# Stage borders of a two-block network: where the second feed-forward tile is converted, and what stands behind the norms

## The chip, the core and the metric

The kernel runs on one core of one Trainium2 chip. The metric is the device time of one execution in microseconds (us), the median of three runs. The engines of a core run beside each other, each works through its own instructions in a fixed order, and they wait for each other by semaphores: TensorE (PE, with its weight load PEld), VectorE (DVE), ScalarE (ACT), GpSimd (POOL), and SyncE (SP), which here issues the weight DMAs.

## The reference

256 tokens of width 1024 go through two transformers of two layers each, in fp32. Each layer is a chain of sub-blocks, and each sub-block begins with an RMS norm and a shift and scale that come from a condition vector. What bears on the change:

```python
mod = (cond @ mod_w[l] + mod_b[l]).reshape(B, 9, D)
h = modulate(rmsnorm(x, norm_g[l, 0]), mod[:, 0], mod[:, 1])
x = x + 0.5 * mod[:, 2][:, None, :] * swiglu(h, ffn_w1[l, 0], ffn_w2[l, 0])
...                       # a mixer (LRU and attention, or NSA), then a second feed-forward
return rmsnorm(x, final_norm_g)          # ends the first transformer

def swiglu(h, w1, w2):
    a, b = jnp.split(h @ w1, 2, axis=-1)
    return (jax.nn.silu(a) * b) @ w2
```

The second transformer has a mixer of four parts, one dense feed-forward and one mixture of eight experts (top 2, width 3584). The change doesn't touch the experts.

## The kernel before

**fp32 as three products.** A matmul in fp32 is made of three: each operand is split into a rounded part and a rest. For weights, `chunk()` (L273 to L303) does it: SP loads 1 MB into a `w` tile (three buffers in turn), ACT writes the rounded part `h` (L301), DVE the rest `lo` (L302), each in two halves of 128x1024. For activations, `split()` (L318 to L320) writes `hhi` on ACT and `hlo` on DVE.

**Order.** The code is traced with a scheduler that chooses each engine's order. Two means bind it: `high_priority()`, and `keep_in_program_order(i)`, which puts instruction i behind the one of the same engine that was traced before it.

**Norm.** `token(t)` (L394 to L399) takes one half of the tokens (128): ACT squares the two halves of X (L341), DVE and POOL make `rstd` (L343, and a power at L344), DVE scales and shifts (`sp<-X,rstd,gate` L383, `sp<-sp,gate` L384), PE transposes (L553) and `split` writes hhi and hlo. In the first mixer of the second transformer, `rstd2` (L350 to L370) joins the final norm of the first transformer with this norm; the normalized X itself is written by ACT (L368) and POOL (L369).

**Feed-forward.** `ffn()` (L471 to L535) runs five times; the traces name them by their places: ffn00, ffn01 (from 346 us), ffn10, ffn11 and ffnb. The width of 2816 is cut into 11 groups of 256 (`j`). Group 0 goes token half by token half as the norms end: `m_tile` with w1 and w3, then `silu` on ACT (L498) and a product `sa` on DVE (L499), whose transposes (`finish`) wait until group 1 has begun. Groups 1 to 10 use `s_form` (L455), weights stationary, 24 matmuls of 256 columns for each 128 columns of weights. After group j comes the down projection of group j-1 with w2, whose tiles come from the pool `own`.

**Modulation steps.** `step()` advances a generator (L189 to L221) that works out later shifts, scales and gates: each step issues two 512 KB loads (`mw`) on SP and two DVE instructions `macc` (L212), 128x1024 each, which are kept in program order. Steps stand between the pieces of the feed-forward groups, and in the two mixers of the first transformer behind each token half of the first projection.

Of the kernel before, what the change touches and what calls it, by code (L numbers as in the profile page):

```python
# [8 lines left out]
FT = mybir.dt.float32  # L9
FR = mybir.dt.float32r  # L10
BF = mybir.dt.bfloat16
I32 = mybir.dt.int32
AF = mybir.ActivationFunctionType
OP = mybir.AluOpType
# [57 lines left out]
class Kernel:  # L72
# [197 lines left out]
        return self.res[key]  # L270


    def chunk(self, src, k, n, own=None, perm=False):  # L273
        nc = self.nc
        raw = self.turn_of(self.raw)
        if isinstance(raw, tuple):

            rr = [r[:, :k * n // 2] for r in raw]
        else:
            rr = [raw.tile([128, 2048], FT, name="w")[:, :k * n]]  # L280
        kk = k // len(rr)
        for i, r in enumerate(rr):
            nc.sync.dma_start(r.rearrange("p (k n) -> p k n", k=kk), src[:, i * kk:i * kk + kk])
        hv, lv = [(own or self.turn_of(pools)).tile([128, 2048], FR, name=name)[:, :k * n]
                  for pools, name in ((self.hip, "h"), (self.lop, "lo"))]
        if perm:

            cut = lambda z, e: z.rearrange("p (k " + e + " v) -> p a k x v", k=k, x=2, a=2)
            for a in range(2):
                o = [cut(z, "a x")[:, a] for z in (hv, lv)]  # L290
                i = cut(rr[0], "x a")[:, a]
                nc.scalar.activation(o[0], i, AF.Copy)
                nc.vector.tensor_sub(o[1], i, o[0].bitcast(FT))
        parts = 0 if perm else max(self.parts, len(rr))
        for x in range(parts):
            d = k * n // parts
            xs = slice(x * d, x * d + d)
            i = x * len(rr) // parts
            at = x * d - i * kk * n
            r = rr[i][:, at:at + d]  # L300
            nc.scalar.activation(hv[:, xs], r, AF.Copy)  # L301
            nc.vector.tensor_sub(lv[:, xs], r, hv[:, xs].bitcast(FT))  # L302
        return (hv.rearrange("p (k n) -> p k n", k=k), lv.rearrange("p (k n) -> p k n", k=k))  # L303

    @staticmethod
# [44 lines left out]
    def rstd2(self, xg, t):  # L350


        nc = self.nc
        ss = self.small.tile([128, 4], FT, name="ss2")
        rr = self.small.tile([128, 2], FT, name="rstd2")
        for h in range(2):
            hs = slice(h * 512, h * 512 + 512)
            nc.vector.tensor_mul(xg[:, hs], self.X[t][h], self.before[:, hs])
            for i, x in enumerate((self.X[t][h], xg[:, hs])):
                scr = self.ps.tile([128, 512], FT, name="p")  # L360
                nc.scalar.activation(scr, x, AF.Square, scale=1.0 / 32.0, accum_out=ss[:, 2 * i + h:2 * i + h + 1])
        nc.vector.tensor_scalar(rr[:, 0:1], ss[:, 0:1], ss[:, 1:2], EPS, op0=OP.add, op1=OP.add)
        nc.vector.tensor_add(ss[:, 2:3], ss[:, 2:3], ss[:, 3:4])
        nc.vector.scalar_tensor_tensor(rr[:, 1:2], rr[:, 0:1], EPS, ss[:, 2:3], op0=OP.mult, op1=OP.add)
        nc.gpsimd.tensor_tensor(rr, rr, self.mhalf.to_broadcast([128, 2]), OP.pow)
        for h in range(2):
            x = self.X[t][h]
            nc.scalar.activation(x, x, AF.Copy, scale=rr[:, 0:1])  # L368
            nc.gpsimd.tensor_tensor(x, x, self.before[:, h * 512:h * 512 + 512], OP.mult)  # L369
        return rr[:, 1:2]  # L370

    def norm_rows(self, g, sh, t):

# [97 lines left out]
    def ffn(self, name, w1, w3, w2, nkey, gkey, ahead):  # L471
        nc = self.nc
        w1, w3, w2 = self.wview(w1), self.wview(w3), self.wview(w2)
        NG = F // 256
        self.ahead(*ahead)
        sh, g = self.mod(*nkey), self.mod(*nkey[:2], nkey[2] + 1)
        self.ctx_first.close()
        with ExitStack() as ctx:
            wk = self.pool(name, 1, ctx)
            own = self.pool(name + "w", 2, ctx)  # L480
            self.n2 = 9
            c = [self.chunk(w[:, :, 0:256], 8, 256) for w in (w1, w3)]
            h, token = self.norm(g, sh)
            A = self.accs()
            todo, G, late = [], {}, []
            for j in range(NG):
                gh = self.t2(wk, [128, 2, 256], "gh", FR)
                gl = self.t2(wk, [128, 2, 256], "gl", FR)
                if j == 0:

                    for t in range(2):
                        with self.tc.high_priority():
                            token(t)
                        p = self.ps.tile([128, 512], FT, name="p")
                        for i in range(2):
                            self.m_tile(p[:, i * 256:i * 256 + 256], h, c[i], 0, 8, 0, 256, t, True, True)
                        sa = self.t2(wk, [128, 256], "sa")
                        nc.scalar.activation(sa, p[:, :256], AF.Silu)  # L498
                        nc.vector.tensor_mul(sa, sa, p[:, 256:])  # L499

                        def finish(t=t, sa=sa, gh=gh, gl=gl):
                            p = self.transpose4(sa, 2)
                            ts = slice(t * 128, t * 128 + 128)
                            self.split(gh[:, :, ts], gl[:, :, ts], p[:, :256].rearrange("p (k n) -> p k n", k=2))
                        late.append(finish)
                else:
                    c = [self.chunk(w[:, :, j * 256:j * 256 + 256], 8, 256) for w in (w1, w3)]
                    pp = []
                    for i in range(2):
                        p = self.ps.tile([128, 512], FT, name="p")  # L510
                        for t in range(2):
                            self.s_form(p[:, t * 256:t * 256 + 256], h, c[i], t * 128)
                        pp.append(p)
                        for finish in late:
                            finish()
                        late = []
                        if j < NG - 1:
                            self.step()
                    sa = self.t2(wk, [128, 512], "sa")
                    nc.scalar.activation(sa, pp[0], AF.Silu)  # L520
                    nc.vector.tensor_mul(sa, sa, pp[1])
                    self.split(gh, gl, sa.rearrange("p (k n) -> p k n", k=2))
                G[j] = (gh, gl)
                if j == 1:
                    self.late_setup()
                for i in ([j - 1] if j < NG - 1 else [j - 1, j]):
                    if i < 0:
                        continue
                    c = self.chunk(w2[:, 2 * i:2 * i + 2, :], 2, 1024, own)
                    todo += [(G[i], k, c, k) for k in range(2)]  # L530
                if todo:
                    self.down(wk, A, todo, j == 1, j == NG - 1, self.mod(*gkey) if j == NG - 1 else None)
                    todo = []
                if j < NG - 2:
                    self.step()  # L535
# [30 lines left out]
    def mixer0(self):  # L566
        nc = self.nc
        W = self.wview(self.i_mix0_in_w[0])
        with ExitStack() as ctx:
# [49 lines left out]
            def tokens(c0):  # L619
                A = self.accs(2)  # L620
                if not R:
                    c = [weights(c0, kh) for kh in range(2)]
                    for t in range(2):
                        with self.tc.high_priority():
                            token(t)
                        for kh in range(2):
                            self.m_tile(A[t], h, c[kh], 4 * kh, 4, 0, 512, t, kh == 0, kh == 1)
                        self.step()
                        yield
                    return A  # L630
                for kh in range(2):
                    c = weights(c0, kh)
                    self.m_form(A, h, c, 4 * kh, 4, 0, 512, kh == 0, kh == 1)
                    self.step()
                    yield
                return A
# [155 lines left out]
    def mixer1(self):  # L792
# [3 lines left out]
        with ExitStack() as ctx:  # L796
# [7 lines left out]
            for t in range(2):  # L804
                with self.tc.high_priority():
                    token(t)
                for kh in range(2):
                    self.m_tile(A[t], h, c[kh], 4 * kh, 4, 0, 512, t, kh == 0, kh == 1)
                self.step()


            V = [wk.tile([128, 2, 9, 64], FR, name=n) for n in ("vhi", "vlo")]
# [266 lines left out]
    def mixer2(self, l):  # L1079
# [3 lines left out]
        with ExitStack() as ctx:  # L1083
# [31 lines left out]
            def m_proj(c0, name):  # L1115
# [4 lines left out]
                for t in range(2):  # L1120
# [3 lines left out]
                    self.m_tile(A[t], h, c, 0, 8, 0, 256, t, True, True)  # L1124
                    if t == 0:
                        yield
                self.step()
                if name is None:
                    return A
# [575 lines left out]
```

## Time and profile before

| | |
|---|---|
| median of three runs | 2661.75 us (2661.14 to 2663.9) |
| the profiled execution | 2663.27 us, of which the span from first to last instruction is 2661.4 us |
| PE busy | 2555.5 us (96%), 14939 matmuls |
| DVE, ACT, POOL busy | 2170.3 us (82%), 1537.0 us (58%), 207.8 us (8%) |
| mean granted TensorE clock | 0.978 of full speed |
| DMA | 727.33 MB, mean 273 GB/s |

How to read it: PE is busy nearly all of the time, so the kernel's length is the matmuls' time, plus the gaps in PE, plus what a lower clock adds. A gap shows in the timeline as idle time in brackets, with the instruction that ended it. An engine with idle time costs nothing by that alone; what counts is whether PE waits for it at that moment. A stretch's granted clock stands in the table by windows (1.00 is 2.4 GHz, 0.50 is 1.2 GHz).

### The profile page before, as it was taken

The numbers are of one execution on the slowest core, as the hardware profiler recorded it, in microseconds if no ns is written. First come the engines' busy times: TensorE is split into PE (matmuls) and PEld (weight loads), VectorE is DVE, ScalarE is ACT, GpSimd is POOL, SyncE is SP. The second block draws the span as 40 slices with busy tenths as digits, with TensorE's granted clock in tenths as the row PEclk, the third lists the DMA queues.
The fourth block names the chain that finished last, engine by engine and source line by source line (L and its number), as shares of the span: only waits on it lengthen the run. The fifth ranks groups of instructions, "written<-read, shape, count | busy, mean of one in ns | idle before, by whom it ended". The sixth has DMA issues, their size and how long they took to land. (4 is left out here: it accounts for less than half of the span.)

```text
span 2661.4 us, 38016 instructions
## 1 busy us (share of the span) xinstructions
PE 2555.5 (96%) x14939; PEld 2207.7 (83%) x14939; DVE 2170.3 (82%) x2446; ACT 1537.0 (58%) x2026; POOL 207.8 (8%) x236
## 2 busy tenths in 40 slices
PE   8999999999998999899999898999999999999997
PEld 5998789989977899887998776888888887888775
DVE  6877888587478787687886976999999898988887
ACT  3454644444446545455444545777777777777775
POOL 2001200000003100231000221000000000000000
PEclk9999999999999999989999988999999999999999
DMA  9986469769553399454895746999999999999993
GB/s 341 335 310 198 174 228 332 259 216 328 179 199 112 111 320 311 157 184 143 298 323 194 239 156 224 381 347 364 347 375 342 348 350 342 348 351 349 351 343 122
DMA packets 366633, 727.33 MB, mean 273 GB/s; under 512 B 16350, under 2 KB 165072, under 8 KB 366448
## 3 DMA queue, kind: packets, MB, share of 16 engines
q1 hardware_dynamic: 362704, 717.20, 77.0%
q0 software_dynamic: 3712, 7.63, 0.9%
q8 instruction: 119, 1.95, 0.3%
q14 instruction: 66, 0.54, 0.1%
q10 hardware_dynamic: 32, 0.01, 0.0%
HBM read 723.73 MB, written 1.05 MB: 272 GB/s over the span
## 5 line engine op out<-in xcount | busy, mean ns | idle before, releaser
L302 DVE TENSOR_TENSOR lo<-w,h 128x1024 fp32r<-128x1024 f32 (+1 forms) x1062 | 1256.6, 1219 | 254.7 <-ACT h L301 248.2
L301 ACT ACTIVATE h<-w 128x1024 fp32r<-128x1024 f32 (+1 forms) x1062 | 1058.7, 1043 | 551.6 <-PE p L316 173.7
L316 PE MATMUL p<-h,xe 128*128 128x512 f32 x1792 | 574.3, 393 | 0.5 <-DVE X L1565 0.5
L316 PE MATMUL p<-hhi,h 128*128 128x256 f32 x1992 | 571.3, 287 | 0.0
L316 PE MATMUL p<-hlo,h 128*128 128x256 f32 x1992 | 567.8, 285 | 0.0
L316 PE MATMUL p<-hhi,lo 128*128 128x256 f32 x1992 | 567.6, 285 | 0.0
L316 PEld LDWEIGHTS p<-h,xe 128*128 128x128 f32 x1792 | 337.3, 188 | 70.8 <-issue 1.7
L316 PEld LDWEIGHTS p<-hhi,h 128*128 128x128 f32 x1992 | 385.3, 193 | 6.0 <-issue 2.2
L316 PEld LDWEIGHTS p<-hlo,h 128*128 128x128 f32 x1992 | 385.4, 193 | 3.3 <-issue 0.7
L316 PEld LDWEIGHTS p<-hhi,lo 128*128 128x128 f32 x1992 | 385.4, 193 | 0.5 <-issue 0.2
L316 PE MATMUL p<-lo,xe 128*128 128x512 f32 x896 | 354.9, 396 | 3.2 <-DVE lo L302 1.7
L212 DVE SCALAR_TENSOR_TENSOR macc<-mw,cond_c,macc 128x1024 f32<-128x1024 f32 x232 | 303.7, 1309 | 29.4 <-DMA mw<-in_w_ada_dram 12.5
L316 PEld LDWEIGHTS p<-lo,xe 128*128 128x128 f32 x896 | 168.7, 188 | 45.3 <-DVE lo L302 12.5
L316 PE MATMUL A<-lo,gTh 128*128 128x512 f32 x448 | 175.9, 393 | 1.3
L316 PE MATMUL A<-h,gTl 128*128 128x512 f32 x448 | 174.6, 390 | 0.0
L316 PE MATMUL A<-h,gh 128*128 128x512 f32 x440 | 172.8, 393 | 0.0
L316 PE MATMUL A<-lo,gh 128*128 128x512 f32 x440 | 171.3, 390 | 0.0
L316 PE MATMUL A<-h,gl 128*128 128x512 f32 x440 | 170.8, 389 | 0.0
L316 PE MATMUL A<-h,gTh 128*128 128x512 f32 x448 | 166.7, 391 | 0.5 <-ACT gTh L319 0.5
L316 PEld LDWEIGHTS A<-lo,gTh 128*128 128x128 f32 x448 | 84.1, 188 | 23.2 <-DVE lo L302 6.3
L316 PEld LDWEIGHTS A<-h,gTh 128*128 128x128 f32 x448 | 84.1, 188 | 18.4 <-ACT gTh L319 0.9
L316 PEld LDWEIGHTS A<-h,gTl 128*128 128x128 f32 x448 | 84.1, 188 | 17.2
(442 smaller groups left out, 3020.0 us busy)
## 6 DMA issues: line engine op xcount, KB each, us to landing
w<-in_moe_w_dram SPq DMA_DIRECT2D x306, 1024.0 KB, 6.3
w<-in_ffn_w_dram SPq DMA_DIRECT2D x165, 1024.0 KB, 7.5
mw<-in_mod_w_dram SPq DMA_DIRECT2D x144, 512.0 KB, 5.2
mw<-in_w_ada_dram SPq DMA_DIRECT2D x96, 512.0 KB, 5.4
gate<-in_moe_w_dram SPq DMA_DIRECT2D x60, 512.0 KB, 6.2
w<-in_w_in_dram SPq DMA_DIRECT2D x24, 1024.0 KB, 5.4
w<-in_mix_in_w_dram SPq DMA_DIRECT2D x17, 1024.0 KB, 5.3
w<-in_mix_out_w_dram SPq DMA_DIRECT2D x8, 1024.0 KB, 5.5
```

The lines of the kernel that those rows point to most:

```text
L212: i = nc.vector.scalar_tensor_tensor(acc, w, self.cond[blk][:, k:k + 1], acc, op0=OP.mult, op1=OP.add)
L301: nc.scalar.activation(hv[:, xs], r, AF.Copy)
L302: nc.vector.tensor_sub(lv[:, xs], r, hv[:, xs].bitcast(FT))
L316: self.nc.tensor.matmul(out, a[l][ai], b[r][bi], start=start and n == 0, stop=stop and n == 2)
```

## The change

Four edits, all around the borders between stages:

1. In a feed-forward, w3's tile of group 0 takes its h and lo from a pool of its own (`own`, now two pools of one buffer in turn), not from the shared turn; not so in ffn10. `gh` of group 0 is allocated earlier, and the small tiles have 13 buffers in place of 9.
2. The chunks of group 1 are pinned: their ACT and DVE instructions stay behind what was traced before them on these engines, which is group 0's `silu` and `sa` and the modulation step between.
3. In the two mixers of the first transformer the two modulation steps come together behind both token halves.
4. The normalized X of the joined norm is written later and on DVE, by `norm_x()`, once both token halves' first projections are issued: four `scalar_tensor_tensor` of 128x512, pinned, in place of four ACT and four POOL instructions.

```diff
-    def chunk(self, src, k, n, own=None, perm=False):
+    def chunk(self, src, k, n, own=None, perm=False, pin=False):
...
+        own = self.turn_of(own) if own else None
...
-            nc.scalar.activation(hv[:, xs], r, AF.Copy)
-            nc.vector.tensor_sub(lv[:, xs], r, hv[:, xs].bitcast(FT))
+            i = (nc.scalar.activation(hv[:, xs], r, AF.Copy), nc.vector.tensor_sub(lv[:, xs], r, hv[:, xs].bitcast(FT)))
+            if pin:
+                for x in i:
+                    self.tc.keep_in_program_order(x)
...
-        for h in range(2):
-            x = self.X[t][h]
-            nc.scalar.activation(x, x, AF.Copy, scale=rr[:, 0:1])
-            nc.gpsimd.tensor_tensor(x, x, self.before[:, h * 512:h * 512 + 512], OP.mult)
+        self.later.append((t, rr, self.before))
         return rr[:, 1:2]
+    def norm_x(self):
+        for t, rr, gain in self.later:
+            for h in range(2):
+                x = self.X[t][h]
+                i = self.nc.vector.scalar_tensor_tensor(x, x, rr[:, 0:1], gain[:, h * 512:h * 512 + 512], op0=OP.mult, op1=OP.mult)
+                self.tc.keep_in_program_order(i)
...
-            own = self.pool(name + "w", 2, ctx)
-            self.n2 = 9
-            c = [self.chunk(w[:, :, 0:256], 8, 256) for w in (w1, w3)]
+            self.n2 = 13
+            gh = self.t2(wk, [128, 2, 256], "gh", FR)
+            own = [self.pool(name + x, 1, ctx, reuse_waits="tile") for x in "wv"][::-1]
+            c = [self.chunk(w1[:, :, 0:256], 8, 256), self.chunk(w3[:, :, 0:256], 8, 256, None if name == "ffn10" else own)]
...
-                    c = [self.chunk(w[:, :, j * 256:j * 256 + 256], 8, 256) for w in (w1, w3)]
+                    c = [self.chunk(w[:, :, j * 256:j * 256 + 256], 8, 256, pin=j == 1) for w in (w1, w3)]
...
                         for kh in range(2):
                             self.m_tile(A[t], h, c[kh], 4 * kh, 4, 0, 512, t, kh == 0, kh == 1)
-                        self.step()
-                        yield
+                    self.step(2)
+                    yield
...
-                self.step()
+            self.step(2)
...
+                self.norm_x()
                 self.step()
```

DVE at the start of ffn01, from the second half of token half 0's norm on (X_97 is its second half, X_98 and X_99 are token half 1; `lo<-w,h` is a weight's rest, here of w3's group 0). Before:

```order
L383 SCALAR_TENSOR_TENSOR sp<-X_97,rstd,gate 128x512
L302 TENSOR_TENSOR lo<-w,h 128x1024
L425 TENSOR_TENSOR tm<-A,gate 128x512
L384 TENSOR_TENSOR sp<-sp,gate 128x512
L426 TENSOR_TENSOR X_99<-X_99,tm 128x512
L320 TENSOR_TENSOR hlo<-p,hhi 128x4x128
L302 TENSOR_TENSOR lo<-w,h 128x1024
L343 TENSOR_SCALAR rstd<-ss 128x1
L320 TENSOR_TENSOR hlo<-p,hhi 128x4x128
L383 SCALAR_TENSOR_TENSOR sp<-X_98,rstd,gate 128x512
```

And with the change:

```order
L395 SCALAR_TENSOR_TENSOR sp<-X_97,rstd,gate 128x512
L396 TENSOR_TENSOR sp<-sp,gate 128x512
L437 TENSOR_TENSOR tm<-A,gate 128x512
L324 TENSOR_TENSOR hlo<-p,hhi 128x4x128
L438 TENSOR_TENSOR X_99<-X_99,tm 128x512
L324 TENSOR_TENSOR hlo<-p,hhi 128x4x128
L347 TENSOR_SCALAR rstd<-ss 128x1
L395 SCALAR_TENSOR_TENSOR sp<-X_98,rstd,gate 128x512
L395 SCALAR_TENSOR_TENSOR sp<-X_99,rstd,gate 128x512
L396 TENSOR_TENSOR sp<-sp,gate 128x512 x2
L302 TENSOR_TENSOR lo<-w,h 128x1024
```

Both halves of w3's lo moved behind the norm's instructions of both token halves; ffn11 and ffnb read alike.

DVE at the end of group 0 of ffn01 (`sa` is group 0's product, its second one of token half 1; the lo's are those of group 1's w1 and w3 and of group 0's w2). Before:

```order
L302 TENSOR_TENSOR lo<-w,h 128x1024 x3
L499 TENSOR_TENSOR sa<-sa,p 128x256
L302 TENSOR_TENSOR lo<-w,h 128x1024 x2
L499 TENSOR_TENSOR sa<-sa,p 128x256
L212 SCALAR_TENSOR_TENSOR macc<-mw,cond_c,macc 128x1024
L302 TENSOR_TENSOR lo<-w,h 128x1024
L212 SCALAR_TENSOR_TENSOR macc<-mw,cond_c,macc 128x1024
```

And with the change:

```order
L514 TENSOR_TENSOR sa<-sa,p 128x256 x2
L212 SCALAR_TENSOR_TENSOR macc<-mw,cond_c,macc 128x1024 x2
L302 TENSOR_TENSOR lo<-w,h 128x1024 x4
L324 TENSOR_TENSOR gl<-p,gh 128x2x128 x2
L212 SCALAR_TENSOR_TENSOR macc<-mw,cond_c,macc 128x1024
```

The four lo's of group 1 moved from ahead of the last `sa` to behind it and behind two macc's. ffn10, ffn11 and ffnb read alike; in ffn00 no macc stands there. ACT has `silu`, `silu` and then the four h's in the same way.

PE there with the change, from group 0's last eight matmuls on (`p<-hhi,h`, `p<-hlo,h`, `p<-hhi,lo` are group 1's three products, `p<-C,sa` the transposes of group 0's product):

```order
L475 MATMUL p<-h,hlo 128x256 x8
L320 MATMUL p<-hhi,h 128x256
L320 MATMUL p<-hlo,h 128x256
L568 MATMUL p<-C,sa 128x128 x4
L320 MATMUL p<-hhi,h 128x256
L320 MATMUL p<-hlo,h 128x256
L320 MATMUL p<-hhi,lo 128x256
```

Before, the first `p<-hhi,lo` is the third matmul of group 1 and the transposes come later; now two matmuls of the w1 product, the four transposes and two of the w3 product stand ahead of it, and then it.

DVE in the first mixer of the second transformer, behind the second token half's norm, with the change (before, the four rows at L380 are not there):

```order
L324 TENSOR_TENSOR hlo<-p,hhi 128x4x128 x2
L380 SCALAR_TENSOR_TENSOR X_96<-X_96,rstd_10679,lo 128x512
L380 SCALAR_TENSOR_TENSOR X_97<-X_97,rstd_10679,lo 128x512
L380 SCALAR_TENSOR_TENSOR X_98<-X_98,rstd_10738,lo 128x512
L380 SCALAR_TENSOR_TENSOR X_99<-X_99,rstd_10738,lo 128x512
L212 SCALAR_TENSOR_TENSOR macc<-mw,cond_c_112,macc 128x1024
L1171 RECIPROCAL lbt<-lbt 128x2
L302 TENSOR_TENSOR lo<-w,h 128x512
```

The four stand ahead of a macc and of the next weight's lo.

## Rows read from the trace of the kernel before

**Rows 1.** Cores: span and mean granted clock.

```profile
core 0: 2661.4 us, clock 0.978
```

**Rows 2.** Timeline of PE, end of ffn01's group 0 (start, us, instruction, [idle before]).

```profile
365.01 1.12 PE L463 MATMUL p<-h,hlo 128*128 128x256 f32 x8
365.97 0.28 PE L316 MATMUL p<-hhi,h 128*128 128x256 f32 x1
366.09 0.28 PE L316 MATMUL p<-hlo,h 128*128 128x256 f32 x1
```

**Rows 3.** Timeline of ACT, the same stretch.

```profile
366.17 0.38 ACT L498 ACTIVATE sa<-p 128x256 f32<-128x256 f32 x1 [0.82 <-PE p L463]
366.45 2.00 ACT L301 ACTIVATE h<-w 128x1024 fp32r<-128x1024 f32 x2
```

**Rows 4.** Timeline of DVE, the same stretch.

```profile
366.71 0.41 DVE L499 TENSOR_TENSOR sa<-sa,p 128x256 f32<-128x256 f32 x1
367.04 1.28 DVE L212 SCALAR_TENSOR_TENSOR macc<-mw,cond_c,macc 128x1024 f32<-128x1024 f32 x1
368.24 1.21 DVE L302 TENSOR_TENSOR lo<-w,h 128x1024 fp32r<-128x1024 f32 x1
```

**Rows 5.** Timeline of PE, norm at the start of ffn01 and ffn11.

```profile
346.71 0.66 PE L553 MATMUL p<-C,sp 128*128 128x128 f32 x4 [0.46 <-DVE sp L384]
...
350.31 1.12 PE L553 MATMUL p<-C,sp 128*128 128x128 f32 x4 [2.25 <-DVE sp L384]
...
907.50 0.66 PE L553 MATMUL p<-C,sp 128*128 128x128 f32 x4 [2.25 <-DVE sp L384]
```

**Rows 6.** Timeline of DVE, norm at the start of ffn01.

```profile
347.17 0.74 DVE L383 SCALAR_TENSOR_TENSOR sp<-X,rstd,gate 128x512 f32<-128x512 f32 x1
347.84 1.21 DVE L302 TENSOR_TENSOR lo<-w,h 128x1024 fp32r<-128x1024 f32 x1
348.97 0.68 DVE L425 TENSOR_TENSOR tm<-A,gate 128x512 f32<-128x512 f32 x1
349.57 0.68 DVE L384 TENSOR_TENSOR sp<-sp,gate 128x512 f32<-128x512 f32 x1
```

**Rows 7.** Windows: length, busy us of PE, PEld, DVE, ACT, POOL, clock, DMA.

```profile
751.00:757.80 6.80, 6.72 (x32) 5.31 (x32) 6.47 (x9) 3.37 (x5) 0.00 (x0) 1.00 0.69 203
349.50:356.30 6.80, 6.00 (x27) 5.83 (x28) 6.74 (x12) 2.36 (x5) 0.55 (x1) 0.50 0.38 110
909.30:912.70 3.40, 3.36 (x15) 3.36 (x16) 3.33 (x7) 0.00 (x0) 0.55 (x1) 0.50 0.51 130
1107.30:1114.10 6.80, 5.63 (x23) 5.07 (x24) 5.40 (x14) 5.87 (x14) 5.37 (x11) 0.50 0.34 98
1131.20:1138.00 6.80, 6.80 (x30) 6.15 (x30) 6.80 (x8) 3.00 (x5) 3.78 (x3) 0.50 0.57 183
```

**Rows 8.** Timeline of DVE, POOL and PE, second norm of the second mixer.

```profile
745.68 1.27 DVE L212 SCALAR_TENSOR_TENSOR macc<-mw,cond_c,macc 128x1024 f32<-128x1024 f32 x1
...
747.17 1.53 POOL L344 TENSOR_TENSOR rstd<-rstd,mhalf 128x1 f32<-128x1 f32 x1 [0.37 <-DVE rstd L343]
...
750.89 1.23 PE L553 MATMUL p<-C,sp 128*128 128x128 f32 x8 [1.42 <-DVE sp L384]
```

**Rows 9.** Timeline of DVE, POOL and PE, first mixer of the second transformer.

```profile
1104.85 1.15 DVE L384 TENSOR_TENSOR sp<-sp,gate 128x512 f32<-128x512 f32 x1
1105.93 1.75 DVE L426 TENSOR_TENSOR X<-X,tm 128x512 f32<-128x512 f32 x1
...
1103.72 3.42 POOL L369 TENSOR_TENSOR X<-X,lo 128x512 f32<-128x512 f32 x2 [0.83 <-ACT X L368]
...
1106.15 0.63 PE L553 MATMUL p<-C,sp 128*128 128x128 f32 x4 [3.31 <-DVE sp L384]
...
1130.45 0.62 PE L463 MATMUL A<-h,hhi 128*128 128x256 f32 x3 [2.33 <-ACT h L301]
```

**Rows 10.** Windows: ffn01 from group 1 on, columns as in rows 7.

```profile
366.00:440.00 74.00, 74.00 (x525) 69.64 (x524) 66.04 (x64) 32.08 (x40) 3.47 (x5) 1.00 0.95 325
```

More of the change, by code (lines that the diff above doesn't have):

```diff
@@ L365, in rstd2 @@
         nc.gpsimd.tensor_tensor(rr, rr, self.mhalf.to_broadcast([128, 2]), OP.pow)
-        for h in range(2):
-            x = self.X[t][h]
-            nc.scalar.activation(x, x, AF.Copy, scale=rr[:, 0:1])
-            nc.gpsimd.tensor_tensor(x, x, self.before[:, h * 512:h * 512 + 512], OP.mult)
+        self.later.append((t, rr, self.before))
         return rr[:, 1:2]
+    later = []
+    def norm_x(self):
[4 more added lines that the diff above has]
+                self.tc.keep_in_program_order(i)
+        self.later = []
     def norm_rows(self, g, sh, t):
@@ L486, in ffn @@
             for j in range(NG):
-                gh = self.t2(wk, [128, 2, 256], "gh", FR)
+                if j > 0:
+                    gh = self.t2(wk, [128, 2, 256], "gh", FR)
                 gl = self.t2(wk, [128, 2, 256], "gl", FR)
```

## The prediction

> **What bounds the kernel now.** I read the cores first: one core, span 2661.4 us, clock 0.978 [rows 1]. In the page's busy times the reader is to see PE at 96%, so only three things can move the time: gaps in PE, the stretches at half clock, and whatever makes either. I then went through PE's timeline at each stage border and looked up on DVE, ACT and POOL what ended each gap.
>
> At the end of group 0 of a feed-forward the reader is to see no gap: the last eight matmuls of group 0 start at 365.01 and group 1 follows at 365.97, 0.12 us from one matmul to the next [rows 2]. ACT's silu of token half 1 runs after that, at 366.17, and DVE's `sa` at 366.71 [rows 3, 4], so group 0's tail lies beside group 1's matmuls. The other four feed-forwards look the same there.
>
> At the start of ffn01, ffn11 and ffnb there is a gap: transposes of token half 0's second part wait 2.25 us for DVE in the two that are shown [rows 5]. On DVE the weight's `lo` (347.84) and `tm` (348.97) stand between the norm's two steps [rows 6]. Behind the gap the clock is 0.50, from 349.5 to 356.3 and from 909.3 to 912.7 [rows 7].
>
> **Part 1: group 1 pinned behind group 0 (five places).** Nothing is removed; what moves is four h and four lo, behind silu, `sa` and, in four of five places, two macc. Call T the time at which group 1 could begin (365.97 in rows 2). silu ends at T+0.58, `sa` starts at T+0.74, the next DVE instruction at T+1.07. Two macc follow at 1.20 each from start to start (367.04 to 368.24), then the first lo at T+3.47, which takes 1.21: ready at T+4.68 [rows 2 to 4]. ACT's h is no later: behind silu two take 2.00, so the first is done at T+1.5. What PE has until then is four matmuls (0.48) and four transposes (0.66 in rows 5), 1.14 in all; the transposes are work that it did later before, so they count as cover. 4.68 - 1.14 = 3.54 lost, four times: 14.2. In ffn00 no macc stands between: h at T+1.48, lo at T+2.69, minus 1.14: 1.55. Together **+15.7**. The bounds: nothing less than two macc and a lo can stand there (the rows of DVE show no wait), and a macc that waited for its load would only add. What stands behind the waiting matmul is all of PE. DVE's later work is late by the same amount; PE needs w3's lo only 24 x 2 x 0.12 = 5.8 us after w1's, and DVE makes one each 1.2, so there is no second wait.
>
> PE's idle piece in this is from about T+1.7 (both `sa` transposed) to T+4.68, 3.0 us. Gaps of 2.25 and 3.31 [rows 5, 9] are followed by a clock of 0.50, the gap of 1.42 is not [rows 7, 8]. A stretch costs half of PE's busy time in it: 3.0 behind ffn01's gap and 1.7 behind ffn11's, 2.8 and 3.4 at the two in the second transformer [rows 7]. The nearest in kind are the feed-forward's own, mean 2.35; four times: **+9.4**, from 0 to 13.6 (ffn00's idle piece is near 1.0: none).
>
> The Trainium skill (TensorE: Matmul & The Clock Gate, section Why this matters for your kernels) asks for no long idle gaps between bursts of matmuls, because the clock then falls to its lower level and the next burst starts slow. It speaks against this change, which makes four such gaps where none was; the trace agrees, by the 0.50 behind the 2.25 us gap. By the rule the 9.4 is due, without it the sum is smaller by just that.
>
> **Part 2: w3's tile apart (ffn01, ffn11, ffnb).** The lo leaves the chain: 348.97 - 347.84 = 1.13, and `tm` now comes behind the addition: 0.60 more, so the transposes start 1.73 earlier: -5.2 for three [rows 6]. That shortens a gap of 2.25 to 0.5, and the half-clock stretch should go: 3.0, 1.7 and, for ffnb, 1.7 as in ffn11: -6.4. But w3's lo now stands behind the additions of token half 1, and token half 0's w3 matmuls wait for it: a lo of 1.21 each that was hidden, so +3.6 (from 0 to twice that, since the tile has two halves). Together **-8.0**. In ffn10 the tile isn't set apart and the order puts one more lo into the chain: +0.5, from 0 to 1.21.
>
> **Part 3: steps behind both norms (both mixers of the first transformer).** In the second one a macc (745.68) stands ahead of the rstd, the power on POOL takes 1.53 beside the next macc, and PE waits 1.42 for what follows [rows 8]. Both macc leave. I take the whole gap, in the first mixer too: **-2.8**. The four macc then stand together ahead of the next lo; cover is the projection's matmuls, and if it failed, the 2 x 1.20 moved would be lost again at each: bounds -2.8 and +2.0.
>
> **Part 4: X later, on DVE.** ACT's and POOL's multiplications of X leave the chain. Two DVE additions took 1.15 and 1.75 beside POOL's 3.42 [rows 9], where the same kind takes 0.68 alone [rows 6]: 1.5 off the wait. The gap of 3.31 stays over 2.25, so its half-clock stretch stays. Added are four DVE instructions that no row shows; the nearest is 0.74 with a scalar [rows 6]: 3.0 us ahead of a macc and the next weight's lo. That lo is used only as the third block of 24 matmuls, 5.8 us later, which covers it; uncovered it is +3.0. The gap of 2.33 at 1130.45, which waits for an h [rows 9], has its matmuls placed later: between 0 and 1.7 + 3.4 (its half-clock stretch, rows 7); I take the middle, 2.5. Together **-4.0**, from +3.0 to -9.4.
>
> **Sum.** 15.7 + 9.4 + 0.5 - 8.0 - 2.8 - 4.0 = +10.8. From the profiled 2663.3 (span 2661.4 and 1.9 around it) that is 2674.1; the median of the runs lies 1.5 below the profiled one, so 2672.6, forecast 2672.5.
>
> **Rivals.**
> - *The new gaps don't lower the clock.* For it: the idle piece is cut by matmuls and transposes at T+1.2 to T+1.7, and PE is dense before and after. Against it: a piece of 3.0 stays, and 2.25 was enough. +10.8 - 9.4 = +1.4: 2663.2.
> - *Faster: the clock decides at the borders.* The new gaps leave the clock, and all half-clock stretches at the norms go: part 2 without its new wait -11.6, part 4 at its end -9.4, part 3 -2.8, against 15.7 + 0.5: -7.6, or 2654.1. It decides when none of the four new gaps and none of the five norms shows 0.50. Against it: the gap of 3.31 shrinks by only 1.5 there.
> - *The loads fall behind.* Group 2's weights need the buffers that group 1's lo's release, some 5 us later now, and DMA is 0.95 busy over the next 74 us [rows 10], so it has 3.7 us to catch up with. If one 1 MB load at 325 GB/s comes too late in each of four feed-forwards: 4 x 3.2 = 12.9 more: 2685.4. Against it: PE itself is later by 3.5 each, and nothing in ffn01 from 366 to 440 shows PE idle (74.00 of 74.00), so there is slack to use up first.
>
> **Chances.** The forecast 0.48, the clock spared 0.25, faster 0.15, loads behind 0.12. About 0.2% (5.3 us) is what a measurement of this kernel can tell from no change. Slower: the forecast nearly whole and the loads, 0.58; within 0.2%: 0.26; faster: 0.16. The range reaches from near the faster case to the late loads: 2657 to 2686.
>
> **What would show it.** Right: in each of ffn01, ffn10, ffn11 and ffnb a PE gap near 3 us at the third matmul of group 1, ended by DVE's lo, and a clock of 0.50 behind it; the 2.25 us gaps at the norms under 1 us with a clock of 1.00; the waits of 1.42 in the mixers gone; DVE additions of 0.68 where 1.15 and 1.75 stood. Wrong: group 1 begins without a gap; or the gaps are there and the clock holds (first rival); or PE waits for weights in groups 2 to 5 (third).

## The result and the profile after

The changed kernel takes 2679.32 us (median of four runs, 2675.77 to 2682.7) against 2662.62 for the kernel before (2661.14 to 2663.9): a ratio of 1.0067, 95% interval 1.0051 to 1.0084, or 16.7 us more. The forecast was 2672.5, within 2657 to 2686.

PE does the same 14939 matmuls in both profiled executions, so the k-th matmul of one can be set against the k-th of the other. How far the changed kernel's stands behind, over each stretch of the kernel before, is a ledger by place (us, from the two traces):

| stretch of the kernel before | part | forecast | measured |
|---|---|---|---|
| hand-over from group 0 to group 1 in ffn00, ffn01, ffn10, ffn11, ffnb, to 20 us behind it | pin, and the clock behind it | 1.6, 5.9 four times: 25.1 | 2.2, 5.4, 6.7, 5.4, 5.4: 25.1 |
| norms of ffn01, ffn11, ffnb | w3's tile apart | -8.0 | -2.7, -2.3, -1.3: -6.3 |
| norms of ffn10 and ffn00 | the same edit | +0.5 and 0 | +2.0 and +1.0 |
| norms of the first transformer's two mixers | steps behind | -2.8 | -1.8, -1.4: -3.1 |
| 1090 to 1165, the second transformer's first mixer | later X | -4.0 | -0.6 |
| 755 to 902, the rest of the second mixer | not in the sum | 0 | +4.0 |
| 250 to 330, the rest of the first mixer | not in the sum | 0 | -3.0 |

These make 19.1; at 2650 us the changed kernel is 17.3 behind. Most of the difference lies behind ffnb's hand-over: between 1297 and 1303 the changed kernel gets 1.9 back, where the kernel before waits 1.11 us for a modulation and the changed kernel doesn't. The hand-over, timeline of PE of the changed kernel, ffn01 (answers to [rows 2]):

```profile
361.13 1.12 PE L475 MATMUL p<-h,hlo 128*128 128x256 f32 x8
363.67 0.39 PE L320 MATMUL p<-hhi,h 128*128 128x256 f32 x1 [1.42 <-ACT h L302]
363.89 0.28 PE L320 MATMUL p<-hlo,h 128*128 128x256 f32 x1
364.01 0.60 PE L568 MATMUL p<-C,sa 128*128 128x128 f32 x4
365.56 0.39 PE L320 MATMUL p<-hhi,h 128*128 128x256 f32 x1 [0.95 <-ACT h L302]
365.78 0.28 PE L320 MATMUL p<-hlo,h 128*128 128x256 f32 x1
366.83 0.38 PE L320 MATMUL p<-hhi,lo 128*128 128x256 f32 x1 [0.77 <-DVE lo L302]
```

And what ACT and DVE did in it (answers to [rows 3, 4]):

```profile
362.29 0.38 ACT L513 ACTIVATE sa<-p 128x256 f32<-128x256 f32 x1 [1.25 <-PE p L475]
362.57 3.89 ACT L302 ACTIVATE h<-w 128x1024 fp32r<-128x1024 f32 x4
...
362.70 0.42 DVE L514 TENSOR_TENSOR sa<-sa,p 128x256 f32<-128x256 f32 x1 [1.21 <-ACT sa L513]
363.04 2.60 DVE L212 SCALAR_TENSOR_TENSOR macc<-mw,cond_c,macc 128x1024 f32<-128x1024 f32 x2
365.56 4.63 DVE L302 TENSOR_TENSOR lo<-w,h 128x1024 fp32r<-128x1024 f32 x4
```

Group 0's last matmuls begin at 361.13, and from then on silu, h, `sa`, two macc and lo follow in a row, with PE idle in three pieces of 1.42, 0.95 and 0.77: 3.14. Two end with ACT's h and only the last with DVE's lo. Group 1 could have begun at 362.09 (0.96 behind 361.13, as in [rows 2]); lo's product (`p<-hhi,lo`) begins at 366.83, so it took 4.74 where the working had 4.68. When it begins, ffn01, ffn11 and ffnb have lost 3.9 each; 1.5 more is lost behind it at half clock.

The windows of the changed kernel: behind the hand-overs of ffn01, ffn11 and ffnb, behind ffn10's norm and its hand-over, and at the norm of ffn01 (columns as in [rows 7], to which they answer):

```profile
368.00:371.40 3.40, 3.40 (x18) 3.40 (x17) 3.40 (x5) 0.89 (x1) 0.00 (x0) 0.50 0.73 237
552.30:555.70 3.40, 3.40 (x18) 3.40 (x17) 3.32 (x7) 0.12 (x2) 0.55 (x1) 0.50 0.71 204
569.40:576.20 6.80, 6.16 (x28) 6.07 (x29) 6.80 (x8) 2.75 (x5) 0.00 (x0) 0.50 0.85 255
938.00:941.40 3.40, 3.40 (x18) 3.40 (x18) 3.40 (x5) 0.94 (x2) 0.00 (x0) 0.50 0.57 191
1293.00:1296.40 3.40, 3.40 (x18) 3.40 (x18) 3.40 (x5) 1.83 (x2) 0.00 (x0) 0.50 0.67 213
346.00:360.00 14.00, 12.80 (x96) 11.29 (x95) 10.10 (x16) 6.29 (x11) 0.55 (x1) 1.00 0.13 32
```

The clock is 0.50 behind all four hand-overs with macc, and 1.00 at ffn01's norm, where [rows 7] had 0.50. That norm, PE and DVE of the changed kernel (answers to [rows 5, 6]):

```profile
347.49 0.66 PE L568 MATMUL p<-C,sp 128*128 128x128 f32 x4 [0.63 <-DVE sp L396]
...
352.98 1.32 PE L568 MATMUL p<-C,sp 128*128 128x128 f32 x8 [0.29 <-DVE sp L396]
...
345.97 0.74 DVE L395 SCALAR_TENSOR_TENSOR sp<-X,rstd,gate 128x512 f32<-128x512 f32 x1
346.75 0.69 DVE L396 TENSOR_TENSOR sp<-sp,gate 128x512 f32<-128x512 f32 x1
...
353.44 1.22 DVE L302 TENSOR_TENSOR lo<-w,h 128x1024 fp32r<-128x1024 f32 x1
```

The wait of 2.25 is 0.63; at ffn11 and ffnb the same wait is 0.64 and 0.72, and the clock is 1.00 there too. In the second mixer's norm the power on POOL takes 0.57, where [rows 8] had 1.53 beside a macc, and the 1.42 wait for the transposes is gone; in the second transformer's first mixer DVE's addition to X takes 0.69 where [rows 9] had 1.75, and PE waits 2.84 where it waited 3.31:

```profile
755.82 0.57 POOL L348 TENSOR_TENSOR rstd<-rstd,mhalf 128x1 f32<-128x1 f32 x1
...
1121.34 0.69 DVE L438 TENSOR_TENSOR X<-X,tm 128x512 f32<-128x512 f32 x1
...
1131.77 2.73 DVE L380 SCALAR_TENSOR_TENSOR X<-X,rstd,lo 128x512 f32<-128x512 f32 x4
...
1121.57 0.63 PE L568 MATMUL p<-C,sp 128*128 128x128 f32 x4 [2.84 <-DVE sp L396]
```

### The profile page after: what moved, and what is told of

Same layout as the page of the kernel before. It is cut to its first block, busy times and chain, and to the rows that moved or that the text cites. A ratio compares the mean times of both kernels' runs of the same rounds, so it can differ in the third digit from the quotient of the medians.

```text
span 2676.6 us, 38063 instructions
## 1 busy us (share of the span) xinstructions
PE 2560.8 (96%) x14939; PEld 2207.5 (82%) x14939; DVE 2171.0 (81%) x2450; ACT 1536.4 (57%) x2022; POOL 196.7 (7%) x232
```

## The experiments

Each was run in turns with the kernel before on the same chip. The runs of the kernel before lay between 2651.4 and 2668.1 in these, so a single run says little; the ratios are taken over many, and the ledger by place is of one profile each. Half-clock stretches within the mixers come and go from one profile to the next (between 250 and 330 pin-alone is 2.3 and later-X 1.6 ahead of the kernel before, though neither edits anything there; between 755 and 902 pin-alone is 3.3 ahead), so a ledger entry there is worth less than one at a stage border.

**No pin.** The changed kernel with one argument taken out:

```diff
-                    c = [self.chunk(w[:, :, j * 256:j * 256 + 256], 8, 256, pin=j == 1) for w in (w1, w3)]
+                    c = [self.chunk(w[:, :, j * 256:j * 256 + 256], 8, 256) for w in (w1, w3)]
```

> The changed kernel without the pin of group 1; w3's own tile, the steps behind both norms and the later X stay. Theory (the pin makes the loss at the five hand-overs from group 0 to group 1, some 24 us by the trace; the gain at the three norms needs the pin as well, since without it another lo of group 1 takes the freed place in the norm's chain): the gaps at the hand-overs go, the 2.25 us gaps at the norms of ffn01, ffn11 and ffnb come back, and the time is about 3 us under the kernel before: 2657 to 2662. Rival A (the own tile alone frees the norm's chain): 2650 to 2655, with no 2.25 us gaps. Rival B (late loads make part of the loss): over 2664, with PE waiting in groups 2 to 5.

2671.46 us, 1.0043 (1.0028 to 1.0058) of before: slower than my range of 2657 to 2662. The hand-overs lose 0.0 in all five, so the whole loss there was the pin's. The norm of ffn01 in this kernel, PE and DVE:

```profile
348.78 0.66 PE L568 MATMUL p<-C,sp 128*128 128x128 f32 x4 [2.25 <-DVE sp L396]
...
345.64 0.75 DVE L395 SCALAR_TENSOR_TENSOR sp<-X,rstd,gate 128x512 f32<-128x512 f32 x1
346.30 1.22 DVE L302 TENSOR_TENSOR lo<-w,h 128x1024 fp32r<-128x1024 f32 x1
347.44 0.68 DVE L437 TENSOR_TENSOR tm<-A,gate 128x512 f32<-128x512 f32 x1
348.04 0.68 DVE L396 TENSOR_TENSOR sp<-sp,gate 128x512 f32<-128x512 f32 x1
```

The 2.25 is back, with a lo in the same place as in [rows 6]: the scheduler has put a lo in again. The trace doesn't tell whose it is; that it is one of group 1 is argued and not shown: in the changed kernel w3's tile is set apart in the same way, group 1 is pinned, and no lo stands there. So rival A falls, and part 2's gain needs the pin too. The time lies in rival B's range, but its sign is missing: behind group 1's start PE waits for no weight in any of the five feed-forwards, only for modulations (`mw`, 1.11 in ffn01, 2.35 in ffn10, 1.02 in ffnb). What I had not counted are the other parts' losses, which this kernel shows without the pin's: norms of ffn00 and ffn10 +1.5, ffn10 behind it (580 to 640) +3.7, the second mixer's rest +4.6, ffnb's norm +2.5.

**Pin alone.** The kernel before with the pin of group 1 (`pin=j == 1` and `keep_in_program_order`, as in the diff of the change) and nothing else.

> The kernel before with the pin of group 1 alone. Theory: the five hand-overs lose 3.3 and four times 5.3 (3.5 to 3.9 of gap and 1.5 to 1.9 of half clock each), 24 to 25 us, and the gaps at the norms stay: 2684 to 2689. Rival A (the pin has a gain of its own at the norms): 2676 to 2681.

2677.23 us, 1.0065 (1.0047 to 1.0082). The ledger at the hand-overs: 2.2, 6.5, 3.9, 6.3 and 5.4 (to 20 us behind each, as above), 24.3 in all, as expected there. The gap at ffn01's norm stays at 2.24. The total is less than the 2684 to 2689 that I expected; this profile is 2.3 and 3.3 us ahead in the two mixers, where the kernel before has more at half clock, and 1.9 ahead at 1301. By its time the pin alone is as costly as the whole change.

ffn10 is the cheap one, 3.9, because the clock holds there. PE at its hand-over, and the window behind it:

```profile
569.19 0.39 PE L318 MATMUL p<-hhi,h 128*128 128x256 f32 x1 [1.42 <-ACT h L301]
...
571.08 0.39 PE L318 MATMUL p<-hhi,h 128*128 128x256 f32 x1 [0.95 <-ACT h L301]
...
572.30 0.50 PE L318 MATMUL A<-h,gh 128*128 128x512 f32 x1 [0.72 <-ACT gh L321]
```

```profile
573.00:582.00 9.00, 9.00 (x78) 9.00 (x77) 9.00 (x10) 2.29 (x4) 0.00 (x0) 1.00 0.89 294
```

ffn10 of the changed kernel has the same three pieces, 1.42, 0.95 and 0.72, and a clock of 0.50 behind them. So the pieces alone don't decide whether the clock falls.

**Macc behind.** The changed kernel with the step behind group 0 traced behind group 1's chunks:

```diff
                     c = [self.chunk(w[:, :, j * 256:j * 256 + 256], 8, 256, pin=j == 1) for w in (w1, w3)]
+                    if j == 1:
+                        self.step()
...
-                if j < NG - 2:
+                if 0 < j < NG - 2:
                     self.step()
```

> The changed kernel with the modulation step that follows group 0 traced behind group 1's two chunks, so that the two macc stand behind the four lo's. Theory: each of four hand-overs loses 2.4 less (two macc at 1.2), and with idle pieces under 2 us the half-clock stretch behind it (1.5 to 1.9) goes too: 4 x 4.1 = 16 under the changed kernel: 2661 to 2666. Rival (the clock falls all the same): only 9.6 under it: 2668 to 2672. Rival (ACT's h is what PE waits for, not the lo behind the macc): at most 3 under it: 2676 or more.

2670.95 us, 1.0032 (1.0017 to 1.0046) of before, where the changed kernel has 1.0067: some 9 us under it. By the time alone the rival that the clock falls all the same would be right: 2670.95 lies within its 2668 to 2672 and above the theory's 2661 to 2666. The ledger shows otherwise at three of the four places. The hand-overs of ffn01, ffn11 and ffnb lose 2.2 to 2.3 each, with nothing lost at half clock behind them; ffn10 loses 2.2 and, at half clock behind it, 1.5. PE at ffn01's hand-over, and the clock there and at ffn11's and ffn10's:

```profile
365.14 0.39 PE L320 MATMUL p<-hhi,h 128*128 128x256 f32 x1 [1.42 <-ACT h L302]
...
366.40 0.39 PE L320 MATMUL p<-hhi,lo 128*128 128x256 f32 x1 [0.32 <-DVE lo L302]
```

```profile
365.00:372.00 7.00, 6.54 (x53) 6.31 (x53) 6.88 (x7) 5.37 (x8) 0.00 (x0) 1.00 0.49 160
929.00:936.00 7.00, 6.68 (x54) 6.44 (x55) 7.00 (x7) 5.18 (x7) 0.00 (x0) 1.00 0.52 171
567.50:570.90 3.40, 3.40 (x18) 3.40 (x18) 3.40 (x4) 3.40 (x6) 0.00 (x0) 0.50 0.52 158
```

Two pieces, 1.42 and 0.32, and the clock holds at three of the four places; at ffn10 it falls behind the same two. At the three the hand-over loses 3.2 less than in the changed kernel (1.7 of gap, 1.5 of clock) where 4.1 was expected, at ffn10 2.9 less: 12.4 in all, of the 16. The time shows 9 of it; in this profile ffn00's hand-over is 1.5 dearer than in the changed kernel, because the clock falls there too (0.51 from 52.0 to 55.5), behind the same 1.42 and 0.32 that it holds behind in the changed kernel; and the stretch from 1165 to 1256, which the edit doesn't touch, 4.4.

**Behind the norm.** The changed kernel with group 1's chunks traced and pinned right behind token half 1's norm:

```diff
                             token(t)
+                        if t == 1:
+                            c1 = [self.chunk(w[:, :, 256:512], 8, 256, pin=True) for w in (w1, w3)]
...
-                    c = [self.chunk(w[:, :, j * 256:j * 256 + 256], 8, 256, pin=j == 1) for w in (w1, w3)]
+                    c = c1 if j == 1 else [self.chunk(w[:, :, j * 256:j * 256 + 256], 8, 256) for w in (w1, w3)]
```

> The changed kernel with group 1's two chunks traced and pinned right behind token half 1's norm, ahead of group 0's second silu and sa. Theory: the norm's chain stays free (gains of some 6 us at ffn01, ffn11 and ffnb), the steps keep their 3 us, and the hand-overs have no gap: 2651 to 2657, faster than the kernel before by 5 to 11. Rival (the place behind the norm delays silu or the loads): 2660 to 2668, with gaps ended by ACT or DMA in group 1.

2658.58 us, 0.9996 (0.9982 to 1.0009) of before: some 19 us under the changed kernel, and just over the 2651 to 2657 that I expected. The hand-overs lose 0.0 and the norms keep all (-2.7, -2.3, -1.3). It is not the 5 to 11 faster, because ffn10 loses 1.7 at its norm and 3.3 behind it, and the second mixer's rest 2.6.

**The parts alone.** Own tile: the kernel before with w3's own pool, the earlier gh and 13 buffers. Steps: with `step(2)` behind both token halves in both mixers. Later X: with `norm_x()`. Each is its lines of the change's diff.

> The kernel before with w3's own tile, the 13 small buffers and the early gh, and nothing else. Theory (without the pin another lo of group 1 takes w3's place in the norm's chain, as the order of its instructions shows): no gain at the norms of ffn01, ffn11 and ffnb (their 2.25 us gaps stay), some 1 to 3 us lost at the norms of ffn10 and ffnb: same as before or up to 5 slower. Rival (the own tile is what freed the chain): the three gaps fall to 0.6 and the time by 5 to 6.

2665.5 us, 1.0026 (1.0016 to 1.0037): slower, by 6 to 7 us where I expected up to 5. The gap at ffn01's norm is still 2.25. In the ledger 0.3 is lost at each of the three norms, 0.9 at ffn00's and 2.0 at ffn10's, and 1.4 in ffn10 behind it.

> The kernel before with the two modulation steps behind both norms in the two mixers, and nothing else. Theory: the gaps of 1.39 and 1.42 go, -1.8 and -1.4 at the two norms; but in the second mixer, where the traces with this edit all show a wait of 6.3 us for ACT and 3 to 5 us lost between 770 and 900, that loss comes from these four macc standing together: net 0 to +2 slower. Rival (that loss comes from elsewhere): 3 us faster, no wait of 6.3.

2661.25 us, 0.9998 (0.9987 to 1.0010): same. -1.8 and -1.4 at the norms, and +3.9 between 755 and 902. What stands there is read in the combination below.

> The kernel before with the later X on VectorE alone. Theory (all traces with this edit gain 4.5 us up to 1145 in the second transformer's first mixer and lose 5 between 1145 and 1165): both are this edit's, net 0 to +1. Rival (the loss there is of the modulation steps): 4 us faster.

2661.66 us, 1.0011 (1.0000 to 1.0022): no gain. -4.9 from 1090 to 1145, +5.0 from 1145 to 1165. In the kernel before PE waits 2.33 at 1130.45 and runs at 0.50 behind it [rows 7, 9]; with the later X it runs at 1.00 there and meets its waits further on. This kernel's windows, at the old place and the new, and PE there:

```profile
1129.00:1136.00 7.00, 6.51 (x54) 6.24 (x52) 6.14 (x7) 4.57 (x6) 2.52 (x2) 1.00 0.71 248
1143.00:1150.00 7.00, 6.24 (x24) 5.31 (x25) 6.56 (x15) 4.34 (x9) 1.76 (x2) 0.51 0.62 204
```

```profile
1141.57 0.73 PE L248 MATMUL p<-mw,ones 128*128 128x512 f32 x2 [1.12 <-ACT mw L238]
1143.51 1.22 PE L470 MATMUL A<-lo,hhi 128*128 128x256 f32 x4 [1.21 <-DVE lo L302]
```

The gain is given back 15 us later, in two waits and another half-clock stretch.

**Combination.** Behind the norm, with ffn10's pools, gh and group 1 as in the kernel before and X on ACT and POOL as before.

> The version with group 1 pinned behind the second norm, with ffn10 left as in the kernel before (but for the scheduler's choice) and X normalized on ACT and POOL as before. Theory: the gains of some 6 at three norms and 3 at the two mixers' norms stay, ffn10's norm loses nothing, the loss at 1145 to 1165 and the gain before it go: 2652 to 2657, 4 to 9 faster than before. Rival (the loss in the second mixer is of the steps and eats it): 2656 to 2660.

2655.09 us, 0.9980 (0.9969 to 0.9990): faster than the kernel before. ffn10's norm gains 0.8 now. The second mixer still loses: PE and DVE of this kernel in its attention, and then the same place in the kernel before:

```profile
814.66 1.12 PE L577 MATMUL p<-C,qz 128*128 128x128 f32 x4 [6.27 <-ACT qz L867]
...
808.03 1.92 DVE L302 TENSOR_TENSOR lo<-w,h 128x1024 fp32r<-128x1024 f32 x1 [0.31 <-ACT h L302]
809.87 2.06 DVE L212 SCALAR_TENSOR_TENSOR macc<-mw,cond_c,macc 128x1024 f32<-128x1024 f32 x1
811.85 0.68 DVE L976 TENSOR_REDUCE mx<-p 128x4 f32<-128x512 f32 x1
```

```profile
818.10 1.11 PE L553 MATMUL p<-C,qz 128*128 128x128 f32 x4 [4.12 <-ACT qz L843]
...
813.88 1.39 DVE L212 SCALAR_TENSOR_TENSOR macc<-mw,cond_c,macc 128x1024 f32<-128x1024 f32 x1 [1.01 <-DMA mw<-in_mod_w_dram]
815.19 0.17 DVE L884 TENSOR_TENSOR cst<-cst,gt 128x16 f32<-128x16 f32 x1
815.27 0.68 DVE L952 TENSOR_REDUCE mx<-p 128x4 f32<-128x512 f32 x1
```

A lo and a macc, both slow at 1.92 and 2.06, now stand ahead of the row maxima that ACT and then PE wait for. This wait is 6.3 in all six kernels with both steps behind the second mixer's norms and 4.1 in the six without, the kernel before among them; between 755 and 902 the first six lose 2.6 to 4.6, the others between 0 and -3.3.

**Steps in one mixer, and in none.** The combination with `self.step()` per token half again in the second mixer, and in both.

> The combination (group 1 pinned behind the second norm, ffn10 and X as in the kernel before) with the steps behind both norms in the first mixer alone; the second mixer has its steps as before. Theory (the steps that come later in the second mixer fall into its attention, where PE waits for DVE: a wait of 6.3 in place of 4.1): the 1.4 at its norm is given back, the 3 to 4 us lost between 770 and 900 go, 2 to 3 faster than the combination: 2651 to 2654 beside 2655. Rival (that loss is of the clock and not of the steps): 1.4 slower than it: 2656 to 2657.

2653.98 us, 0.9978 (0.9967 to 0.9990). The second mixer's wait is 4.14 again, and its stretch from 770 to 902 gives 3.1 where the combination loses 4.0. Not all of these 7.1 are the steps': pin-alone, which has the steps as before, is 3.3 ahead there too. By the ratios to the kernel before the gain over the combination is 0.0002, some 0.5 us, less than the 2 to 3 and within what the intervals leave open; the profiled execution (2648.41) is at the low end of its runs.

> The same combination with the steps of both mixers as in the kernel before: only w3's own tile and group 1 behind the second norm are left. Theory (the steps of the first mixer are worth 1 to 2): the three norms' gain of some 6 alone: 2652 to 2655. Rival (the norm's gain is what the whole combination had, less what is lost on the way): same as the combination, 2655.

2654.14 us, 0.9984 (0.9974 to 0.9994): the norms' gains alone are nearly all. The three combinations can't be told apart by their times. PE at ffn01 in the version with the first mixer's steps, from the norm's transposes to group 1:

```profile
344.95 0.66 PE L577 MATMUL p<-C,sp 128*128 128x128 f32 x4 [0.63 <-DVE sp L399]
...
358.58 1.12 PE L478 MATMUL p<-h,hlo 128*128 128x256 f32 x8
359.54 0.28 PE L320 MATMUL p<-hhi,h 128*128 128x256 f32 x1
359.66 0.28 PE L320 MATMUL p<-hlo,h 128*128 128x256 f32 x1
```

Both at once: the short wait at the norm, and no gap at the hand-over.

## Why the prediction was right, step by step

**Part 1** carried the sign. Its chain came out at 4.74 against 4.68, and chain and clock together at 25.1, as worked out. That the sum fits so well is luck: the loss up to lo's product was 3.9 and not 3.54 (2.2 and not 1.55 in ffn00), the half clock behind it 1.5 at three places and some 2.8 in ffn10 (its 6.7 less pin-alone's 3.9), not 2.35, and the two errors, some 2 us each, cancel. The no-pin run shows that all of it is the pin's; the macc-behind run shows that the two macc are in it, for 1.7 of gap at each place, and at three of the four places for the clock's share too. The sign that I had named, one gap near 3 ended by lo, is not in the trace: there are three pieces, 1.42, 0.95 and 0.77, because group 1's first matmul needs an h that silu now precedes. I had counted four matmuls as free from T on, and they only move within the chain. The first rival, that cutting the idle piece would spare the clock, is refuted at all four places of the changed kernel, but in pin-alone it came true at ffn10: there the clock held.

**Part 2** had the right mechanism at the norms (0.63 for 2.25, the clock at 1.00), and 1.7 less gain than worked out. Its step "w3's tile apart: the lo leaves the chain" was credited to the wrong edit: it takes the pin as well, as no-pin and own-alone show. The 2.0 at ffn10's norm and 1.0 at ffn00's were sized at 0.5 and 0; a half-clock stretch stands at each, and ffn00's is missing in macc-behind, which has the same lines there and loses nothing.

**Part 3** was right at the norms, -3.1 for -2.8. Its cover was the part that I took on trust: I had it fail at the projection, and in the second mixer it failed in the attention, some 70 us later, for +3.9 in steps-alone.

**Part 4** is the term that was mis-sized: -4.0 forecast, -0.6 measured, +0.1 in the ledger and no gain in the time when alone. The additions did fall from 1.75 to 0.69, but the wait behind them by 0.5 (3.31 to 2.84) and not by 1.5. The clock held at 1130, but the next waits then ended the gain. The sum missed by 6.5 in the ledger (17.3 against 10.8): parts 2 and 4 and the second mixer make it 1.7 + 1.5 + 1.0 + 3.4 + 4.0 more, part 3, the first mixer and the places outside the table 0.3 + 3.0 + 1.8 less.

**The third rival** had no part: in all five feed-forwards of the changed kernel PE waits for no weights (no wait over 0.25 us) behind the start of group 1 (ffn01 has -0.2 from 380 to 530 in the ledger).

Open: why ffn10 loses between 580 and 640 in the six kernels that have w3's own tile in the other feed-forwards and no gaps at the hand-overs. PE waits there for the end of a modulation (ACT's `mw`): 1.7 to 2.4 in four of them, with a half-clock stretch of 3.4 us behind it and 3.3 to 3.7 lost, and 1.3 in the other two, with no such stretch and 1.4 lost. Why the modulation comes later there than in the kernel before no run takes apart. Nor was it tried what each half-clock stretch within the mixers hangs on.

## What to carry to other kernels

A pin in a scheduled program has two ends. It keeps work out of the critical chain ahead of it, and it puts that work behind whatever was traced last on its engine; trace the pinned work right behind the chain that it is to spare, and not behind the consumer of what runs beside it. Taking one filler out of a chain gains nothing while the scheduler has another one ready, so look at the order again, not at the line that was moved. And background work that is moved to a later place still has to run somewhere: look for the next place where the matmul engine waits for its engine.

## What the runs showed that was not expected

- The clock fell to 0.50 behind the idle pieces of a hand-over with macc ahead (1.42, 0.95 and a third of 0.4 to 0.8 us), or within the later of them, at seven of the eight places in the changed kernel and pin-alone, and held at 1.00 at the eighth. Behind 1.42 and 0.32 it held at five of seven places (ffn00 in the changed kernel and pin-alone, ffn01, ffn11 and ffnb in macc-behind) and fell at two (ffn00 and ffn10 in macc-behind). What decides it between equal pieces, no run shows. The kernel before had it at 1.00 behind a single gap of 1.42 [rows 7, 8].
- POOL's power of 128 values took 0.57 us with no macc beside it and 1.53 beside one, which reads two operands of 128x1024; DVE's addition of 128x512 took 0.69 alone and 1.75 beside POOL's multiplication. The Trainium skill (SBUF — State Buffer, section Who interferes with whom) has it that a VectorE instruction with two SBUF inputs contends with a GpSimd instruction that reads SBUF, for a shared pair of ports that is an exclusive lock; the two rows agree with it.
